# A macaron layer with two FFNs: more joint FFN blocks, token products last, theta per head, inverse roots without reciprocals

## The chip, the cores and the metric

The kernel runs on one NeuronCore of a Trainium2 chip. The metric is the device time of one execution in microseconds; smaller is better. Three runs of the kernel before gave 2110.48, 2112.5 and 2111.97 us (median 2111.97). All data is float32; large products are done in TensorE's `fp32r` format.

## The reference

One decoder layer on 1024 tokens of 1024 features. It adds half a SwiGLU FFN to `x`, then a mixer, then half a second FFN, and ends with an RMSNorm.

```python
x = x + 0.5 * swiglu(rms_norm(x, ffn1_norm), ffn1_w_gate, ffn1_w_up, ffn1_w_down)   # D_FF = 2816 = 22 x 128
x = x + hybrid_mixer(rms_norm(x, mix_norm), w_in, ...)
x = x + 0.5 * swiglu(rms_norm(x, ffn2_norm), ffn2_w_gate, ffn2_w_up, ffn2_w_down)
return rms_norm(x, final_norm)

def swiglu(h, w_gate, w_up, w_down):
    return (silu(h @ w_gate) * (h @ w_up)) @ w_down
```

The mixer projects `h @ w_in` to 3808 columns. Four HGRN2 heads of 128 (columns q, f, i, g) do gated linear recurrence in chunks of 64 tokens, each output normed over its head: `o * rsqrt(mean(o*o) + 1e-6)`. Eight RWKV-7 heads of 64 (columns r, k, v and low-rank columns for decay, `a` and gate) run a delta-rule recurrence; their key is divided by its length, `kk / max(sqrt(sum(kk*kk)), 1e-12)`, and their output is group-normed, `(y - mean) * rsqrt(var + 64e-5)`. Both halves are joined and multiplied by `w_out`. All mixing is causal.

## The kernel before

Features lie on the 128 partitions and tokens along the free dimension. The 1024 tokens are two blocks of `TB` = 512. Each large product is done in three passes (`mm3`, lines 101 to 103): weights and operands are split into a rounded part `hi` and a rest `lo` (`split`, lines 69 and 70: ScalarE rounds, VectorE subtracts), and `w.hi*x.hi + w.hi*x.lo + w.lo*x.hi` is summed in PSUM. Weights come from DRAM in pieces of 128 x 512 (`w_raw`), are split, and are used once or twice.

The order in time is:

1. `ffn_both`, FFN1. The first 10 of 22 FFN column blocks (`ALONE`) are done for token block 0 alone, the other 12 (`BOTH`) for both token blocks jointly by `unit`. A unit treats [gate, up] x [two halves of the features] x [two token blocks] as a 2 x 2 matrix product and does it with 7 half products instead of 8. It needs sums and differences of the weight pieces, made by VectorE (lines 287 to 298), and of the operands, made once per FFN by `Versions.first` and `Versions.rest`; the latter are `jobs`, taken one at a time from block 3 on. The down products of a group go to both token blocks, and `down` adds them onto the residual (line 459).
2. `project_in` for token block 0: first the token-major products (`tokens`, lines 587 to 589), which give the i columns and the 160 low-rank columns as tokens x columns, the low-rank part then transposed back; then 24 column products r, k, v and f, q, g (evacuated in line 648). From the sixth on, the first RWKV pairs are prepared (`early`).
3. `mixer` for block 0, in between the large products of what follows: `rwkv_pair` (keys, decays, gram matrices), `rwkv_solve` (a triangular inverse, theta, by VectorE), `rwkv_chain` (8 chunks one after the other), `rwkv_post` (group norm), twice, and four `hgrn_head`. It stores its outputs to DRAM (`od`).
4. `ffn` for block 1, its 10 blocks of FFN1 that were left out, then `project_in` and `mixer` of block 1.
5. For each token block: `project_out` (loads `od` by `out_operands`, multiplies by `w_out`, adds the parked residual) and `ffn` with all 22 blocks of FFN2 in six `GROUPS`. The final norm of block 0 is done in the middle of block 1's output projection; block 1's last group is done token-major by `Finish`, which norms and stores.

No order is written out by hand for the engines. A list scheduler orders the instructions of each engine by priority: a place in the program, moved ahead by `AHEAD` = 6000 for loads, splits and evacuations, by `SOON` = 20000 for the RWKV work, by `AHEAD - LATER` for the operand versions. All DMAs but a few go through SP's queue. Buffers are rings (`hp` for normed operands, `ft`, `w_raw`, `v` for operand versions, `sh`, `sr`, `po` for the mixers, PSUM rings `psf` 3, `hq` 2, `rq` 2, `ry` 1); rings of a later `stage` lie over those of the earlier one, in the order of their declaration.

An inverse root is `rsqrt` (lines 122 and 123: ScalarE square root, VectorE reciprocal); `rwkv_pair` has its own in lines 792 and 793. In a step of `rwkv_chain`, `z` is copied into a block-diagonal tile `zbd` by ScalarE (907) and VectorE (908), two products with theta and all 128 rows give `u` (913), and ScalarE copies it (914).

Of the kernel before, what the change touches and what calls it, by code (L numbers as in the profile page):

```python
# [15 lines left out]
P = 128  # L16
D = 1024
# [19 lines left out]
NTOK = 256  # L37
TOK_AT = 0
# [139 lines left out]

def ffn(E, xs, g, wgu, wdn, r=None, finish=None, groups=GROUPS, onto=None):

    nc = E.nc
    end = sum(groups[-1])
# [14 lines left out]
    def gate(pg, pu, half):  # L197
        with E.tc.high_priority(AHEAD):
# [16 lines left out]
    for f0, nf in groups:  # L215
        a = []
        last = finish and f0 + nf == NF
        if last:
            w_last = finish.weights(E, wdn, f0, nf)
        for f in range(f0, f0 + nf):  # L220
# [8 lines left out]
            a.append(gate(*late[:2], last))  # L229
            if wait and f == 1:  # L230
                late.append(product(f, 1))
                a.append(gate(*late[2:], last))
            late = []
        if last:
            finish(E, xs, a, w_last)
            return
# [10 lines left out]
    return xs  # L247
# [105 lines left out]
class Gate(Parts):  # L353


    def silu(self, t):
        with self.E.tc.high_priority(AHEAD):
            self.E.nc.scalar.activation(out=t, in_=t, func=AF.Silu)
# [6 lines left out]
    def c21(self, x):  # L365
        E, V = self.E, self.E.nc.vector
        with E.tc.high_priority(AHEAD):
            V.tensor_tensor(out=self.t0, in0=x, in1=self.t0, op=ALU.mult)
# [4 lines left out]
class Versions:  # L373
# [41 lines left out]
def ffn_both(E, x0, x1, g, wgu, wdn):  # L415


    nc = E.nc
# [31 lines left out]
    def gated(f):  # L450
        use = Gate(E)
# [12 lines left out]
    jobs = [lambda: r.append(rstd_of(E, x1))] + [lambda k=k: v.rest(x1, r[1], k) for k in range(HK)]  # L464
    ahead = None
    for f0, nf in ALONE:
        a = []
        for f in range(f0, f0 + nf):
# [6 lines left out]
            if f == 1:  # L475
                v.first(x0, r[0])
# [8 lines left out]
    for f0, nf in BOTH:  # L485
        a += [gated(f) for f in range(f0 + len(a), f0 + nf)]
        if f0 + nf < NF:
# [6 lines left out]
            continue  # L494
        for hb, xs in enumerate((x0, x1)):
            for d in range(KD):
                down(xs, d, wd(d, f0, nf), [h[hb] for h in a], "psf")


class Finish:  # L500
# [5 lines left out]
    def weights(self, E, wdn, f0, nf):  # L506
        nc = E.nc
        self.gain = []
        for h in range(2):
            t = E.ev.tile([P, TB + 1], F32, name="ev")[:, 0:TB]  # L510
            nc.sync.dma_start(out=t, in_=self.nf_row[:, h * TB:(h + 1) * TB].broadcast_to([P, TB]))
            self.gain.append(t)
        w = []
        with E.tc.high_priority(AHEAD):
            for h in range(2):
                for f in range(f0, f0 + nf):
                    raw = E.wraw.tile([P, 512], F32, name="w_raw")
                    nc.sync.dma_start(out=raw.rearrange("p (d c) -> p d c", c=P), in_=wdn[4 * h:4 * h + 4, :, f * P:(f + 1) * P].rearrange("d p c -> p d c"))
                    w.append(split(E, raw, E.sh.tile([P, TB], F32R, name="sh"), E.sr.tile([P, TB + 1], F32R, name="sr")[:, 0:TB]))
        return [w[:nf], w[nf:]]  # L520

    def __call__(self, E, xs, a, w):
        nc = E.nc
        E.idle = ["hq", "hq", "rq", "rq", "ry"]
        for t in range(TB // P):
# [3 lines left out]
            for h in range(2):  # L529
# [7 lines left out]
                sq = E.rs.tile([P, TB], F32, name="rs")  # L537
# [26 lines left out]
def project_in(E, b, xs, g, win, wtok, midway, early):  # L564
# [10 lines left out]
    def tokens(w_cols, n, banks, hooks={}):  # L575

        each = TB // P // len(banks)
        ps = [getattr(E, name).tile([P, TB], F32, name=name) for name in banks]
        ps = [p[:, i * n:(i + 1) * n] for p in ps for i in range(each)]
        for k in range(KD):  # L580
            if k in hooks:
                hooks[k]()
            w = load_piece(E, w_cols[:, k * n:(k + 1) * n])
            for t, p in enumerate(ps):
                x = h[k][:, t * P:(t + 1) * P]
                opens, closes = k == 0 and t % each == 0, k == KD - 1 and t % each == each - 1
                nc.tensor.matmul(p, x.hi, w.hi, start=opens, stop=False)
                nc.tensor.matmul(p, x.lo, w.hi, start=False, stop=False)
                nc.tensor.matmul(p, x.hi, w.lo, start=False, stop=closes)
        return ps  # L590

    def evacuate(p, t, c, dst):
        n = p.shape[1]
        e = E.ft.tile([P, TB], F32, name="ft")[:, 0:n]
        nc.scalar.activation(out=e, in_=p, func=AF.Copy, scale=rt[:, t:t + 1])
        nc.sync.dma_start(out=pd["i"][t * P:(t + 1) * P, dst:dst + n - c], in_=e[:, c:n])
        return e

# [4 lines left out]
    def rms_of_tokens():  # L603
        p = E.psf.tile([P, TB], F32, name="psf")[:, 0:4]
        for t in range(4):
            nc.tensor.matmul(p[:, t:t + 1], r[:, t * P:(t + 1) * P], E.ident[:, 0:1], start=True, stop=True)
        with tc.high_priority(AHEAD):
            nc.vector.tensor_copy(out=rt, in_=p)

    r = None  # L610
    rt = E.rw.tile([P, 4], F32, name="rt")
    first = tokens(wtok[:, 0:KD * NTOK], NTOK, ("hq", "hq"))
    second = tokens(wtok[:, KD * NTOK:], 512 + NLOW + NG - NTOK, ("rq", "rq", "ry", "psf"), {TOK_AT: rms, TOK_AT + 3: rms_of_tokens})
    lows = [E.psf.tile([P, TB], F32, name="psf") for _ in range(2)]
# [26 lines left out]
    for ci, name in enumerate(order):  # L641
# [13 lines left out]
        if ci == 5:  # L655
            early(pd, low)
# [634 lines left out]
```

## Time and profile before

| what | before |
|---|---|
| median of three runs | 2111.97 us |
| the profiled execution, its time and its span | 2111.52 us, 2108.6 us |
| TensorE busy | 2061.7 us, 11144 matmuls |
| VectorE busy | 1395.8 us, 2369 instructions |
| ScalarE busy | 954.3 us, 1562 instructions |
| mean granted TensorE clock | 0.995 |
| read from HBM | 197.77 MB |

The span goes from the first to the last instruction; the time adds what lies around it. A matmul's busy time is its latency, and matmuls overlap, so counts and starts of matmuls say more than busy times. Lines are those of the kernel before.

### The profile page before, as it was taken

How to read it: one execution, taken by the hardware profiler on the slowest of the kernel's cores; microseconds unless marked ns; L12 is line 12 of the kernel's file. 1: busy time of each engine (PE TensorE's matmuls, PEld its weight loads, DVE VectorE, ACT ScalarE, POOL GpSimd, SP SyncE). 2: the span in 40 equal slices, each digit the busy share in tenths (PEclk: the TensorE clock that was granted, in tenths of full speed). 3: DMA queues.
4: the chain of work that ended last, by engine and by line, in shares of the span. 5: the costliest groups of instructions: out<-in, count | busy, mean ns of one | idle time of the engine just before them, and what ended most of it. 6: DMA issues, size and time to landing. Idle time of an engine off the chain costs nothing.

```text
span 2108.6 us, 29995 instructions
## 1 busy us (share of the span) xinstructions
PE 2061.7 (98%) x11144; PEld 1674.6 (79%) x11144; DVE 1395.8 (66%) x2369; ACT 954.3 (45%) x1562; POOL 37.8 (2%) x68
## 2 busy tenths in 40 slices
PE   8999999999999999999999998999999999999998
PEld 6788888888877778776877776877888888888887
DVE  7876645455677978886677789966444675444553
ACT  6443423233556756544556556544332453322333
POOL 0000000001010000000000000000000000000000
PEclk9999999999999999999999999999999999999999
DMA  6332211213544543343645532433332453333331
GB/s 195 89 96 61 60 51 52 64 46 120 163 151 150 168 123 111 109 110 106 195 133 157 165 97 91 118 98 91 95 97 90 139 180 96 100 95 98 98 114 66
DMA packets 156962, 233.81 MB, mean 111 GB/s; under 512 B 36976, under 2 KB 54384, under 8 KB 156816
## 3 DMA queue, kind: packets, MB, share of 16 engines
q1 hardware_dynamic: 155952, 230.55, 36.5%
q8 instruction: 87, 1.43, 0.3%
q10 hardware_dynamic: 864, 1.36, 0.2%
q14 instruction: 59, 0.48, 0.1%
HBM read 197.77 MB, written 34.08 MB: 110 GB/s over the span
## 4 chain that ended last, share of the span: by engine, by line
PE 89%; DVE 5%; ACT 2%; issue 2%; DMA 1%; SPq 0%; ACTq 0%; DVEq 0%
PE psf L103 23%; PE psf L102 23%; PE psf L101 23%; PE hq L103 2%; PE hq L101 2%; PE hq L102 2%; PE rq L824 1%; DVE w_lo L70 1%; PE rq L102 1%; PE rq L103 1%; PE rq L101 1%; PE rq L913 1%; PE rq L917 1%; PE rq L906 1%; ACT w_hi L69 1%
## 5 line engine op out<-in xcount | busy, mean ns | idle before, releaser
L69 ACT CAST w_hi<-w_raw 128x512 fp32r<-128x512 f32 (+3 forms) x668 | 404.0, 606 | 875.4 <-PE psf L102 666.7
L70 DVE TENSOR_TENSOR w_lo<-w_raw,w_hi 128x512 fp32r<-128x512 f32 (+3 forms) x668 | 442.0, 666 | 190.7 <-ACT w_hi L69 187.9
L103 PE MATMUL psf<-h_hi,w_lo 128*128 128x512 f32 x1312 | 517.3, 395 | 7.9 <-DVE w_lo L70 7.9
L101 PE MATMUL psf<-h_hi,w_hi 128*128 128x512 f32 x1312 | 518.6, 395 | 3.5 <-ACT rs L122 2.2
L102 PE MATMUL psf<-h_lo,w_hi 128*128 128x512 f32 x1312 | 518.9, 396 | 0.0
L103 PEld LDWEIGHTS psf<-h_hi,w_lo 128*128 128x128 f32 x1312 | 247.0, 188 | 63.9 <-DVE w_lo L70 11.8
L101 PEld LDWEIGHTS psf<-h_hi,w_hi 128*128 128x128 f32 x1312 | 247.0, 188 | 57.7 <-ACT rs L122 2.7
L102 PEld LDWEIGHTS psf<-h_lo,w_hi 128*128 128x128 f32 x1312 | 247.1, 188 | 52.8 <-issue 1.9
L101 PE MATMUL psf<-v,w_hi 128*128 128x512 f32 x488 | 190.1, 389 | 1.6 <-ACT v L69 1.1
L103 PE MATMUL psf<-v,w_lo 128*128 128x512 f32 x488 | 189.9, 389 | 0.0
L102 PE MATMUL psf<-v,w_hi 128*128 128x512 f32 x488 | 189.9, 389 | 0.0
L101 PE MATMUL psf<-a_hi,w_hi 128*128 128x512 f32 x408 | 159.7, 392 | 0.5 <-ACT a_hi L69 0.5
L102 PE MATMUL psf<-a_lo,w_hi 128*128 128x512 f32 x408 | 159.4, 391 | 0.0
L103 PE MATMUL psf<-a_hi,w_lo 128*128 128x512 f32 x408 | 158.8, 390 | 0.0
L246 DVE SCALAR_TENSOR_TENSOR xp<-psf,xp 128x512 f32<-128x512 f32 x112 | 77.0, 689 | 79.5 <-PE psf L103 78.8
L101 PEld LDWEIGHTS psf<-v,w_hi 128*128 128x128 f32 x488 | 91.6, 188 | 21.5 <-ACT v L69 1.5
L102 PEld LDWEIGHTS psf<-v,w_hi 128*128 128x128 f32 x488 | 91.6, 188 | 19.1
L103 PEld LDWEIGHTS psf<-v,w_lo 128*128 128x128 f32 x488 | 91.6, 188 | 18.9
L101 PEld LDWEIGHTS psf<-a_hi,w_hi 128*128 128x128 f32 x408 | 76.4, 188 | 17.4 <-ACT a_hi L69 0.9
L102 PEld LDWEIGHTS psf<-a_lo,w_hi 128*128 128x128 f32 x408 | 76.6, 188 | 16.0 <-DVE a_lo L70 0.2
L103 PEld LDWEIGHTS psf<-a_hi,w_lo 128*128 128x128 f32 x408 | 76.5, 188 | 15.8
L209 DVE TENSOR_TENSOR ft<-psf,ft 128x512 f32<-128x512 f32 x50 | 34.4, 689 | 56.5 <-PE psf L103 56.4
(400 smaller groups left out, 2875.5 us busy)
## 6 DMA issues: line engine op xcount, KB each, us to landing
w_raw<-in_wgu_dram SPq DMA_DIRECT2D x304, 256.0 KB, 3.1
w_raw<-in_wd_dram SPq DMA_DIRECT2D x134, 256.0 KB, 2.7
w_raw<-in_win_dram SPq DMA_DIRECT2D x96, 256.0 KB, 3.0
w_raw<-in_wout_dram SPq DMA_DIRECT2D x32, 256.0 KB, 2.8
w_raw<-in_wd_dram SPq DMA_DIRECT2D x24, 192.0 KB, 2.3
park<-xp SPq DMA_DIRECT2D x16, 256.0 KB, 2.0
xp<-park SPq DMA_DIRECT2D x16, 256.0 KB, 3.5
ft<-od SPq DMA_DIRECT2D x16, 256.0 KB, 3.6
```

The costliest lines, as they stand in the source:

```text
L69: nc.scalar.copy(out=hi, in_=raw)
L70: nc.vector.tensor_tensor(out=lo, in0=raw, in1=f32(hi), op=ALU.subtract)
L101: E.nc.tensor.matmul(ps, w.hi, x.hi, start=start and i == 0, stop=False, **on)
L102: E.nc.tensor.matmul(ps, w.hi, x.lo, start=False, stop=False, **on)
L103: E.nc.tensor.matmul(ps, w.lo, x.hi, start=False, stop=(i == n - 1), **on)
L209: nc.vector.tensor_tensor(out=s, in0=pu, in1=s, op=ALU.mult)
L246: nc.vector.scalar_tensor_tensor(out=xs[d], in0=p, scalar=0.5, in1=xs[d], op0=ALU.mult, op1=ALU.add)
L824: PE.matmul(gps[hh][:, c, :], bk[r, c0 + c, :, :], g.ra[r, jj, c0 + c, :, :], start=True, stop=True)
L906: PE.matmul(z[r, jj, :], ra[r, jj, cc, 1, :], M[r, jj, :], start=False, stop=jj == 1, tile_position=(hh * C, hh * C))
L913: PE.matmul(u[C:P, jj, :], E.theta[:, jj, cc, :], E.zbd[:, jj, :, :], start=True, stop=True, tile_position=(0, C))
L917: PE.matmul(m[r, jj, :], bkt[:, cc, jj, r], uv[:, cc, jj, r], start=True, stop=True, tile_position=(0, hh * C))
```

## The change

- `ALONE` has 8 blocks instead of 10 and `BOTH` 14 instead of 12. FFN2 now uses the same scheme: token block 0 does its 8 blocks by `ffn` right after its output projection; then, in a stage of its own, the output projection of block 1 and `ffn_both` with block 1 as the first and block 0 as the second token block. Block 0's residual before FFN2 is stored to DRAM (`mid`) and loaded again for its operand versions; its inverse root `r` is kept. Block 0's final norm now comes between the last down products and `Finish`, whose group has 4 blocks instead of 3.
- The first stage declares its rings as `v, a, xb, wraw, ft` instead of `xb, ft, wraw, a, v`.
- In `project_in` the low-rank columns are done first and feature-major (two products with 64 and 96 output rows), and the token-major i products last, in two passes of two token tiles that load the weights each.
- In `rwkv_chain` theta is applied per head: four products of 64 x 64 instead of two with the block-diagonal tile; their result is copied half by ScalarE and half by VectorE.
- In the mixers' three norms `rsqrt_step` takes the place of root and reciprocal: logarithm, exponential, square, and one Newton step on VectorE. Its factor -0.5 is folded into constants (`onorm2`, `k_k2`) or the next operation.

```diff
-GROUPS = ((0, 4), (4, 4), (8, 4), (12, 4), (16, 3), (19, 3))
-ALONE = ((0, 4), (4, 4), (8, 2))
-BOTH = ((10, 4), (14, 4), (18, 4))
+ALONE = ((0, 4), (4, 4))
+BOTH = ((8, 4), (12, 4), (16, 2), (18, 4))
...
+def rsqrt_step(E, y, z, scratch):
+    A, V = E.nc.scalar, E.nc.vector
+    A.activation(out=y, in_=z, func=AF.Ln)
+    A.activation(out=y, in_=y, func=AF.Exp, scale=-0.5)
+    A.activation(out=scratch, in_=y, func=AF.Square)
+    V.tensor_tensor(out=z, in0=scratch, in1=z, op=ALU.mult)
+    V.scalar_tensor_tensor(out=y, in0=z, scalar=-3.0, in1=y, op0=ALU.add, op1=ALU.mult)
...
-    first = tokens(wtok[:, 0:KD * NTOK], NTOK, ("hq", "hq"))
-    second = tokens(wtok[:, KD * NTOK:], 512 + NLOW + NG - NTOK, ("rq", "rq", "ry", "psf"), {TOK_AT: rms, TOK_AT + 3: rms_of_tokens})
+    for i, (at, m, dst) in enumerate(((NG, NLOW, lraw), (0, NG, sgl))):
+        p = E.psf.tile([P, TB], F32, name="psf")[0:m]
+        for k in range(KD):
+            if k % 3 == 0:
+                w = load_piece(E, wtok[:, k * NL:min(k + 3, KD) * NL])
+            c = k % 3 * NL + at
+            if i == 0 and k == 1:
+                rms()
+            for n, (u, x) in enumerate(((w.hi, h[k].hi), (w.hi, h[k].lo), (w.lo, h[k].hi))):
+                nc.tensor.matmul(p, u[:, c:c + m], x, start=k + n == 0, stop=k == KD - 1 and n == 2)
... (after the 24 column products)
+    for two in ((0, 1), (2, 3)):
+        ps = [E.psf.tile([P, TB], F32, name="psf") for _ in two]
+        for k in range(KD):
+            w = load_piece(E, wtok[:, KD * NL + k * TB:KD * NL + (k + 1) * TB])
+            for t, p in zip(two, ps):
+                ... (three passes of 128 x 512)
...
-    rsqrt(E, sq, ss, P, E.eps)
+    z, sq, tmp = s2(), s2(), s2()
+    V.tensor_scalar(out=z, in0=ss, scalar1=1.0 / P, scalar2=EPS, op0=ALU.mult, op1=ALU.add)
+    rsqrt_step(E, sq, z, tmp)
...
-    A.activation(out=sq, in_=sq, func=AF.Sqrt)
-    V.reciprocal(out=sq, in_=sq)
+    z, sq, tmp = sq, tk(s2()), tk(s2())
+    rsqrt_step(E, sq, z, tmp)
...
-            A.copy(out=E.zbd[0:C, :, 0, :], in_=z[0:C])
-            V.tensor_copy(out=E.zbd[C:P, :, 1, :], in_=z[C:P])
+            A.copy(out=E.zs[0:C], in_=z[0:C])
+            V.tensor_copy(out=E.zs[C:P], in_=z[C:P])
...
-            for jj in range(2):
-                PE.matmul(u[C:P, jj, :], E.theta[:, jj, cc, :], E.zbd[:, jj, :, :], start=True, stop=True, tile_position=(0, C))
-            A.copy(out=uv[C:P, cc, :, :], in_=u[C:P])
+            for jj, hh, r in heads:
+                PE.matmul(u[r, jj, :], E.theta[r, jj, cc, :], E.zs[r, jj, :], start=True, stop=True, tile_position=(hh * C, hh * C))
+            A.copy(out=uv[C:P, cc, :, 0:C], in_=u[0:C])
+            V.tensor_copy(out=uv[C:P, cc, :, C:P], in_=u[C:P])
...
-    with stage(xb=8, ft=6, wraw=7, a=8, v=28):
+    with stage(v=28, a=8, xb=8, wraw=7, ft=6):
...
-        for b in range(NB):
-            o = out_operands(E, ods[b])
-            xs = project_out(E, o, parks[b], wout, lambda: b and final(b - 1, xs))
-            ffn(E, xs, E.n2, wgu2, wd2, finish=Finish(nf_row, out_last) if b + 1 == NB else None)
+        o = out_operands(E, ods[0], "hp")
+        xs = project_out(E, o, parks[0], wout, "xp")
+            mid = to_dram(xs, "mid")
+        xs, r = ffn(E, xs, E.n2, wgu2, wd2)
+    with stage(v=28, a=8, xb=8, wraw=7, ft=6, rw=1):
+        o = out_operands(E, ods[1], "v")
+        xb = project_out(E, o, parks[1], wout, "xb")
+        ffn_both(E, xb, xs, E.n2, wgu2, wd2, of_first, r, Finish(nf_row, out_last), lambda: final(0, xs))
```

More of the change, by code (lines that the diff above doesn't have):

```diff
@@ L195, in product, with gate @@
         return p
-    def gate(pg, pu, half):
+    def gate(pg, pu):
         with E.tc.high_priority(AHEAD):
@@ L214, in ffn @@
     late = []
-    for f0, nf in groups:
+    for f0, nf in ALONE:
         a = []
-        last = finish and f0 + nf == NF
-        if last:
-            w_last = finish.weights(E, wdn, f0, nf)
         for f in range(f0, f0 + nf):
@@ L450, in gated @@
     def gated(f):
-        use = Gate(E)
+        use = Gate(E, 0.5 if finish and f >= BOTH[-1][0] else None)
         unit(E, [wgu[f, :, j, i * TB:(i + 1) * TB] for j in range(2) for i in range(2)], v, use)
@@ L494, in ffn_both @@
             continue
+        if finish:
+            w_last = finish.weights(E, wdn, f0, nf)
         for hb, xs in enumerate((x0, x1)):
+            if finish and hb == 0:
+                continue
             for d in range(KD):
                 down(xs, d, wd(d, f0, nf), [h[hb] for h in a], "psf")
+        if finish:
+            then()
+            finish(E, x0, [h[0] for h in a], w_last)
 class Finish:
@@ L507, in weights @@
         nc = E.nc
[L508 to L512, printed above, removed]
+        t = E.v.tile([P, 2, TB], F32, name="v")
+        nc.sync.dma_start(out=t.rearrange("p h c -> p (h c)"), in_=self.nf_row.broadcast_to([P, D]))
+        self.gain = [t[:, h, :] for h in range(2)]
         w = []
@@ L573, in project_in @@
     pd = {"i": E.dram.tile([TB, 512], F32, name="pd_i")}
[L575 to L597, printed above, removed]
     def rms():
@@ L656, in project_in @@
             early(pd, low)
+    rt = E.rw.tile([P, 4], F32, name="rt")
+    p = E.psf.tile([P, TB], F32, name="psf")[:, 0:4]
+    for t in range(4):
+        nc.tensor.matmul(p[:, t:t + 1], r[:, t * P:(t + 1) * P], E.ident[:, 0:1], start=True, stop=True)
+    with tc.high_priority(AHEAD):
+        nc.vector.tensor_copy(out=rt, in_=p)
+    for two in ((0, 1), (2, 3)):
[3 more added lines that the diff above has]
+            for t, p in zip(two, ps):
+                x = h[k][:, t * P:(t + 1) * P]
+                nc.tensor.matmul(p, x.hi, w.hi, start=k == 0, stop=False)
+                nc.tensor.matmul(p, x.lo, w.hi, start=False, stop=False)
+                nc.tensor.matmul(p, x.hi, w.lo, start=False, stop=k == KD - 1)
+        with tc.high_priority(AHEAD):
+            for t, p in zip(two, ps):
+                e = E.ft.tile([P, TB], F32, name="ft")
+                nc.scalar.activation(out=e, in_=p, func=AF.Copy, scale=rt[:, t:t + 1])
+                nc.sync.dma_start(out=pd["i"][t * P:(t + 1) * P], in_=e)
     return low, sg, pd, ahead
@@ L993, in out_operands, with project_out @@
             nc.sync.dma_start(out=t, in_=od[k])
-            hi = E.hp.tile([P, TB], F32R, name="h_hi")
-            lo = E.hp.tile([P, TB], F32R, name="h_lo")
-            o.append(split(E, t, hi, lo))
+            if ring == "v":
+                o.append(part(E, t, ring))
+            else:
+                o.append(split(E, t, E.hp.tile([P, TB], F32R, name="h_hi"), E.hp.tile([P, TB], F32R, name="h_lo")))
     return o
-def project_out(E, o, xpark, wout, midway):
+def project_out(E, o, xpark, wout, ring):
     nc = E.nc
@@ L1066, in mixer_constants @@
     G.memset(E.theta, 0.0)
[L1067 to L1068 removed]
+    E.zs = k.tile([P, 2, C], F32, name="zs")
     wraw = E.sh.tile([P, TB], F32, name="sh")[0:64]
```

100 lines of the change are left out of this document (43 added, 57 removed).

## The prediction

> **What bounds the kernel now.** I read the page's parts 1, 2 and 4 first, then the timeline of the tensor engine where nothing disturbs it.
>
> ```profile
> span 2108.6 us, 29995 instructions
> PE 2061.7 (98%) x11144; PEld 1674.6 (79%) x11144; DVE 1395.8 (66%) x2369; ACT 954.3 (45%) x1562; POOL 37.8 (2%) x68
> PE   8999999999999999999999998999999999999998
> PE 89%; DVE 5%; ACT 2%; issue 2%; DMA 1%; SPq 0%; ACTq 0%; DVEq 0%
> 1849.65 0.39 PE L102 MATMUL psf<-h_lo,w_hi 128*128 128x512 f32 x1
> 1864.83 0.39 PE L103 MATMUL psf<-a_hi,w_lo 128*128 128x512 f32 x1
> 219.49 0.69 DVE L368 TENSOR_TENSOR ft<-psf,ft 128x512 f32<-128x512 f32 x1
> 238.53 0.69 DVE L368 TENSOR_TENSOR ft<-psf,ft 128x512 f32<-128x512 f32 x1
> ```
>
> TensorE is busy in every slice and holds 89% of the chain that ended last, so the question is how many matmuls go and which idle stretches come or go. The reader must not use the 0.39 us: that is one matmul's latency, and its neighbours overlap it. From 1849.65 to 1864.83 stand 68 matmuls in a row: 15.18 / 67 = 0.2266 us each. The two L368 rows are the ends of two joint units of FFN1, 19.04 us apart = 84 x 0.2267: a joint block runs at the pure matmul pitch.
>
> **1. Sixteen more joint blocks: -43.4 us.** A block of 128 FFN columns done for each token block alone takes 2 x 2 x 8 x 3 = 96 gate and up matmuls, 21.75 us; the joint unit takes 7 x 4 x 3 = 84, 19.04 us by the row above. The change makes 2 more in FFN1 (12 to 14) and 14 in FFN2 (none so far): 16 x 2.71 = 43.4. The down matmuls stay the same in number. Weight pieces and their splits become fewer (7 splits and 4 additions instead of 8 splits for a unit, one load of down weights for two products), and the evacuation grows a little.
>
> ```profile
> 40.00:60.00 20.00, 17.47 (x75) 13.56 (x74) 19.97 (x33) 13.79 (x24) 0.00 (x0) 1.00 0.33 93
> 60.00:80.00 20.00, 18.75 (x82) 14.88 (x81) 17.03 (x23) 9.15 (x13) 0.00 (x0) 1.00 0.27 79
> 120.00:140.00 20.00, 20.00 (x90) 16.57 (x89) 18.30 (x30) 9.82 (x17) 0.00 (x0) 1.00 0.31 92
> 340.00:360.00 20.00, 20.00 (x90) 16.57 (x89) 12.78 (x20) 9.20 (x16) 0.00 (x0) 1.00 0.21 54
> 2080.00:2108.00 28.00, 22.07 (x112) 17.72 (x110) 9.79 (x22) 11.17 (x26) 0.00 (x0) 0.98 0.20 75
> ```
>
> Columns: window, length, busy time of PE, PEld, DVE, ACT, POOL, granted clock, DMA share. In the joint stretch (340 to 360) VectorE has 7 of 20 us to spare, so the new units in FFN2 are hidden under TensorE. Where a joint FFN begins they are not: at 40 to 80 VectorE prepares the 16 operand versions and TensorE loses 2.53 + 1.25 = 3.8 us. FFN2 now gets such a beginning: **+3.8**. The first joint unit now follows block 7 rather than block 9, while at 120 to 140 VectorE was still 18.3 of 20 busy with the versions' last part: I take **+2** for each FFN, +4 (0, when the unit's first 5.4 us of products that need only the early versions cover it; 10, about one part's VectorE work, when not). In FFN2 that part also has to load the other block's `mid` tiles again and takes 5 of the 6 `ft` buffers; this lies within the same bound. The final norm of block 0 moves to the tail, beside the last token-major products, where DMA is 0.20 and VectorE a third busy: **+1**, 0 to 4.
>
> **2. Token products last, low-rank columns first: -4.6 and -2.**
>
> ```profile
> 544.42 0.80 PE L587 MATMUL hq<-w_hi,h_hi 128*128 128x256 f32 x2 [3.79 <-ACT h_hi L173]
> 579.36 0.40 PE L101 MATMUL hq<-h_hi,w_hi 128*128 128x512 f32 x1
> L829 PE MATMUL rq<-ident,t 128*128 128x128 f32 x64 | 9.7, 274 | 0.0
> 540.00:560.00 20.00, 15.89 (x105) 15.06 (x104) 15.69 (x28) 12.56 (x25) 0.18 (x1) 0.83 0.79 240
> ```
>
> Now: 34.94 us from the first token product to the first column product, in each of two blocks 69.9 (taken the same for the second). After: 48 narrow-output matmuls with 512 columns and 96 token matmuls with 512 columns, 144 x 0.2266 = 32.6, twice 65.3. The 16 transposes of the low-rank part go: at most 16 x 0.274 = 4.4, I take 2 because they overlap others. No new wait: the low products pass in 10.9 us, and their evacuation needs `r`, but the two borrowed banks carry two column products, 10.9 us, meanwhile.
>
> **3. The pools' order in the first stage: -3.8 us.** The 544.42 row shows TensorE idle for 3.79 us until ScalarE wrote `h_hi`. In the old order the new `hp` pool lies over `xb`, which the last down products still write and which then has to be stored. In the new order it lies over `v`, read last by the joint units; the split can run under the 96 last down products (21.8 us). If that cover fails the term is 0.
>
> **4. Theta per head: 0, -9 to +11.**
>
> ```profile
> 968.74 0.45 PE L906 MATMUL rq<-mst,ra 64*64 64x64 f32 x8
> 970.02 0.65 PE L913 MATMUL rq<-zbd,theta 128*64 128x128 f32 x4
> 969.29 0.26 ACT L907 COPY zbd<-rq 64x128 f32<-64x128 f32 x1 [0.52 <-PE rq L906]
> 969.58 0.29 DVE L908 COPY zbd<-rq 64x128 f32<-64x128 f32 x1 [1.01 <-ACT zbd L907]
> 970.70 0.37 ACT L914 COPY uv<-rq 64x256 f32<-64x256 f32 x1 [1.15 <-PE rq L913]
> ```
>
> Per step of the chain, 32 in all: the theta products take 0.65 us, and per head they have the shape of L906, 0.45: -0.20. Their copy, 0.37 on ScalarE alone, becomes one on ScalarE and one on VectorE. Side by side they take 0.29 (-0.28 a step, -9); one after the other, as L907 and L908 run on one PSUM tile, 0.58 (+0.01 a step). I take the latter, the nearest row; a VectorE that is busy when its copy comes adds up to half of a 0.69 us operation, 32 x 0.35 = +11.
>
> **5. No reciprocals: -4, 0 to -8.**
>
> ```profile
> L123 DVE RECIPROCAL po<-po 128x512 f32<-128x512 f32 x8 | 26.8, 3350 | 3.6 <-ACT po L122 3.6
> L123 DVE RECIPROCAL sh<-sh 128x512 f32<-128x512 f32 x8 | 26.7, 3343 | 1.7 <-ACT sh L122 1.7
> L793 DVE RECIPROCAL sr<-sr 128x512 f32<-128x512 f32 x8 | 26.7, 3338 | 1.0 <-ACT sr L792 1.0
> L941 DVE TENSOR_TENSOR po<-po 128x512 f32<-128x512 f32 x8 | 5.5, 689 | 0.0
> L797 DVE SCALAR_TENSOR_TENSOR sr<-sr,vec 128x512 f32<-128x512 f32 x8 | 6.0, 748 | 0.0
> L139 ACT ACTIVATE ft<-xp 128x512 f32<-128x512 f32 x56 | 33.8, 626 | 14.0 <-DVE ft L141 8.1 <-DVE xp L1012 3.8 <-DVE xp L246 1.6
> L686 ACT ACT_TABLE_LOAD x8 | 10.3, 1283 | 0.1
> L718 ACT ACT_TABLE_LOAD x6 | 7.7, 1283 | 0.1
> PE psf L103 <- DVE w_lo L70: 7.9, 8, 1.7
> ```
>
> VectorE loses 24 reciprocals of 3.34 and gains 24 x (0.69 + 0.75) + 16 x 0.69: 80.2 - 45.6 = 34.6 us less. What TensorE gets of that is bounded by its waits for a split weight piece, 7.9 us in all; I take half. ScalarE gains a second and a third pass (2 x 0.63) and, since L718's exponential reloads its table after L686's logarithm, one more load of 1.28: 24 x 2.54 = 61 us, on an engine that is 45% busy. The step is not shorter for the one who waits: 1.28 + 0.63 + 3.34 = 5.3 before, about 2 x 1.28 + 3 x 0.63 + 0.69 + 0.75 = 5.9 after (root, logarithm and square taken as long as L139's pass).
>
> The Trainium skill says in "ScalarE: Activation LUTs", section "Table sets: the hidden batching unit", that logarithm and exponential share a set, so the pair costs one load. By that rule ScalarE would do 24 x 1.28 = 31 us less and the sum would stay; the second block's mixers would end some 8 x 1.28 = 10 us earlier, and I would give the first rival 12 instead of 18 in 100. The L718 row speaks against it: the kernel pays a load there now.
>
> **6. The cover of the second block's mixers: +4, 0 to +25.** This is the term I know least.
>
> ```profile
> L758 SPq DMA_DIRECT2D od<-sh x8: 326/327/327, 776.9 to 1405.3; - x8
> L945 SPq DMA_DIRECT2D od<-po x8: 319/326/327, 809.5 to 1468.3; - x8
> 1181.93 0.69 DVE L648 TENSOR_TENSOR ev<-psf,rs 128x512 f32<-128x512 f32 x1
> L102 PE MATMUL psf<-h_lo,w_hi 128*128 128x512 f32 x209 | 86.2, 413 | 0.0
> L102 PE MATMUL psf<-a_lo,w_hi 128*128 128x512 f32 x62 | 24.1, 389 | 0.0
> 1181.00:1468.00 287.00, 281.17 (x2172) 217.50 (x2172) 229.57 (x426) 151.98 (x250) 3.88 (x5) 0.99 0.36 105
> od<-po SPq DMA_DIRECT2D x8, 256.0 KB, 2.1
> ft<-od SPq DMA_DIRECT2D x16, 256.0 KB, 3.6
> ```
>
> From the last column products (1181.9) to the mixers' last store (1468.3) TensorE issues 3 x (209 + 62) = 813 large matmuls, 184 us, between the mixers' small ones; they come from the first output projection and the first block's FFN2, which has plenty left at 1468. After the change the first block's FFN2 alone has only 8 blocks: 8 x 72 = 576 matmuls, with 192 of the output projection and the 96 token products moved there 864, 196 us. Nothing else can run until the second output projection gets its operands: store and load (2.1 + 3.6 us) and eight splits (8 x 0.69 on VectorE), 11 us, some 10 since the first heads are loaded before. So 196 against 184 + 10: the cover just holds, and with the mixers' jitter I take +4. SP's queue carries those loads ahead of the output weights, and both stand behind the last store.
>
> **Sum.** -43.4 + 3.8 + 4 + 1 - 4.6 - 2 - 3.8 + 0 - 4 + 4 = -45.0. The profiled execution took 2111.5 (span 2108.6 and 2.9 around it), 0.5 under the median shown: 2111.5 - 45.0 = 2066.5, so **2066 us**.
>
> **The rivals.** (a) The cover falls short. For it: the balance in 6 and VectorE busy 229.6 of 287 us there. Against it: of the 34.6 us that VectorE saves, those after 1181 (four heads, four norms and two pairs, 8 x 1.2 + 2 x 1.9 = 13.4, less 16 x 0.29 for theta copies) shorten the queue that the mixers wait in. A shortfall of 25 us in place of the 4 gives 2066 - 4 + 25, and a slow clock comes on top: in the 540 row, after 3.79 us idle, the clock is 0.83 over 20 us, 3.4 us lost. That is 2090, chance 18. The Trainium skill ("TensorE: Matmul & The Clock Gate", "Part 1: The HAM clock gate") has half clock after one idle window of about 3.4 us until about 3.4 us of work have passed, which would make that loss 1.7 and this rival 2089.
>
> (b) Slower than before, by the HGRN heads: they need the token products, which now come last. Those are 22 us of large products in a stretch where such products get 184 of 287 us, so the heads end 34 us later, at 1405 + 34 = 1439, still ahead of the 1468 of the RWKV norms. Should they be pushed behind all RWKV work instead, each us past the cover is a us of idle TensorE; from 45 + 4 - 3.4 = 46 us on, past 1468 + 46 = 1514, the kernel is slower than before: 2112 to 2130. Chance 5.
>
> (c) VectorE's relief counts for more: in the stretch from 1181 to 1468 the mixers' small matmuls and waits take 287 - 184 = 103 us; an eighth of it less in both blocks is 25 us, 2041. For it speaks VectorE's 80% there, against it that the waits for a split piece sum to only 7.9. Chance 17.
>
> (d) The change doesn't do in FFN2 what it does in FFN1, for lack of `ft` buffers or VectorE, and its joint blocks run at the alone pace: 14 x 2.71 = 38 back, 2104. The 340 row speaks against it; chance 3. The forecast has the other 57.
>
> **How the numbers follow.** 2066 is the likeliest case. Its own range, the ends of terms 1 to 6 that are not rivals and never all at one side: chain -9 to +11, reciprocals -4 to +4, beginnings -9 to +9, cover -4 to +10: 2050 to 2082. With (c) and the shortfalls up to 25 us the range is 2041 to 2091, leaving out (b), (d) and the rims of the others. 0.2% is 4.2 us, about what a measurement of this kernel can tell: (b) is slower, almost nothing falls within 4.2 us of 2112, everything else is faster: 0.93, 0.02, 0.05.
>
> **What would show it.** FFN2's units end 19.04 us apart with TensorE full (1); TensorE not idle for over 1 us ahead of block 0's first low-rank product (3); the theta copies staggered or side by side (4); no reciprocal in the mixers and about 24 more table loads (5); between the last `od` store of block 1 and the first product on it, TensorE busy (6). A clock under 1.00 and idle TensorE just ahead of the second output projection would make the prediction wrong upward; TensorE fuller than now through both mixers, downward.

## The result, and the profile after

The changed kernel takes 2131.1 us (median of four runs, 2130.0 to 2140.3) against 2111.2: ratio 1.0105, 95% interval 1.009 to 1.012. It is 20 us slower where 45 us less were forecast. Its profiled run is the longest of the four (2140.3), so the trace read here shows some 9 us more than the median.

The page's summary misleads: TensorE is 97% busy, against 98% before. What helps is to cut the span at two events, the first product on the low-rank operand (the mixers' recurrence begins; L779 before, L777 after) and the last `od` store (L756 the HGRN heads, L946 the RWKV norms). Rows of the lines' own lists (min/median/max ns, first and last start):

```profile
L779 PE MATMUL rq<-low,w x8: 477/483/501, 588.1 to 1274.7; 96*128 96x512 f32 x8
```
```profile
L777 PE MATMUL rq<-low,w x8: 472/480/502, 588.5 to 1317.7; 96*128 96x512 f32 x8
L756 SPq DMA_DIRECT2D od<-sh x8: 319/326/327, 877.3 to 1492.2; - x8
L946 SPq DMA_DIRECT2D od<-po x8: 319/326/327, 816.7 to 1518.0; - x8
```

The windows between these events (length, then busy time and number of instructions of PE, PEld, DVE, ACT and POOL, then the granted clock, the DMA share and GB/s), before and then after:

```profile
0.00:588.00 588.00, 570.66 (x2552) 473.36 (x2552) 364.72 (x571) 243.60 (x415) 14.17 (x29) 0.99 0.31 92
588.00:1468.00 880.00, 857.93 (x5790) 678.62 (x5791) 691.73 (x1278) 487.69 (x779) 23.60 (x40) 0.99 0.42 126
1468.00:2108.00 640.00, 633.14 (x2804) 522.60 (x2802) 339.38 (x522) 222.96 (x369) 0.00 (x0) 1.00 0.35 107
```
```profile
0.00:588.00 588.00, 573.91 (x2504) 468.84 (x2504) 383.32 (x598) 247.01 (x413) 12.88 (x26) 1.00 0.30 88
588.00:1518.00 930.00, 886.36 (x5810) 685.13 (x5811) 669.43 (x1342) 550.96 (x852) 27.85 (x41) 0.97 0.42 127
1518.00:2138.00 620.00, 606.98 (x2656) 497.71 (x2654) 381.61 (x590) 235.24 (x405) 0.00 (x0) 0.99 0.26 81
1760.00:2000.00 240.00, 240.00 (x1061) 198.72 (x1060) 125.70 (x191) 76.22 (x129) 0.00 (x0) 1.00 0.17 51
```

The part behind the mixers is 20 us shorter, and FFN2's joint blocks keep TensorE full there (last row). The part ahead is as long as it was. The mixers' span grew by 50 us, with VectorE's work down by 22 us and ScalarE's up by 63. No engine is full in that span: TensorE idles 44 of 930 us and runs at clock 0.97, VectorE is 72% busy. I take it for a chain of latencies with large products laid between; e4, e5 and e16 below test that. What part of the 50 us the lower clock has was not separated.

Each run below, cut in the same way (us; the median and ratio are of all its runs, the other columns of its profiled one; "ahead" to the first low-rank product, "span" to the later of the two last stores):

| run | median | ratio (95%) | ahead | last RWKV / HGRN store | span | behind |
|---|---|---|---|---|---|---|
| before | 2111.2 | | 588 | 1468 / 1405 | 880 | 640 |
| after | 2131.1 | 1.0105 (1.009-1.012) | 588 | 1518 / 1492 | 930 | 621 |
| e1 | 2122.6 | 1.0055 (1.004-1.007) | 589 | 1481 / 1502 | 914 | 621 |
| e2 | 2136.7 | 1.0128 (1.0113-1.0143) | 583 | 1490 / 1517 | 934 | 623 |
| e3 | 2129.4 | 1.0089 (1.0074-1.0104) | 584 | 1475 / 1512 | 928 | 618 |
| e4 | 2109.8 | 0.9996 (0.9987-1.0006) | 611 | 1492 / 1430 | 881 | 616 |
| e5 | 2076.4 | 0.9836 (0.9821-0.985) | 581 | 1459 / 1398 | 878 | 615 |
| e6 | 2165.0 | 1.0249 (1.0232-1.0266) | 610 | 1552 / 1485 | 942 | 615 |
| e7 | 2125.3 | 1.0065 (1.005-1.008) | 589 | 1470 / 1505 | 916 | 618 |
| e8 | 2156.0 | 1.02 (1.0174-1.0225) | 589 | 1520 / 1447 | 931 | 637 |
| e9 | 2133.3 | 1.0109 (1.0094-1.0124) | 588 | 1488 / 1426 | 899 | 644 |
| e10 | 2144.0 | 1.0158 (1.0141-1.0175) | 578 | 1468 / 1499 | 920 | 647 |
| e11 | 2140.0 | 1.0145 (1.013-1.0161) | 589 | 1498 / 1434 | 909 | 640 |
| e12 | 2070.2 | 0.9808 (0.9793-0.9823) | 582 | 1462 / 1401 | 880 | 606 |
| e13 | 2150.6 | 1.0195 (1.0178-1.0212) | 573 | 1469 / 1490 | 917 | 658 |
| e14 | 2130.2 | 1.0098 (1.0083-1.0113) | 588 | 1481 / 1454 | 893 | 649 |
| e15 | 2102.5 | 0.9966 (0.9953-0.9979) | 561 | 1458 / 1486 | 926 | 614 |
| e16 | 2067.0 | 0.9796 (0.9781-0.981) | 554 | 1459 / 1397 | 905 | 607 |

### The profile page after: what moved, and what is told of

It is laid out like the page before. It is cut to its first block, busy times and chain, and to the rows that moved or that the text cites. A ratio compares the mean times of both kernels' runs of the same rounds, so it can differ in the third digit from the quotient of the medians.

```text
span 2138.6 us, 29619 instructions
## 1 busy us (share of the span) xinstructions
PE 2067.2 (97%) x10968; PEld 1651.7 (77%) x10968; DVE 1434.4 (67%) x2529; ACT 1033.2 (48%) x1669; POOL 40.7 (2%) x67
## 3 DMA queue, kind: packets, MB, share of 16 engines
q10 hardware_dynamic: 864, 1.36, 0.2%
## 4 chain that ended last, share of the span: by engine, by line
PE 44%; DVE 4%; ACT 3%; issue 2%; DMA 1%; SPq 0%; DVEq 0%; ACTq 0%
PE psf L99 9%; PE psf L100 9%; PE psf L101 9%; PE hq L100 2%; PE hq L101 2%; PE hq L99 2%; PE rq L101 1%; PE rq L100 1%; PE rq L99 1%; DVE w_lo L68 1%; PE rq L822 1%; PE rq L911 1%; PE rq L916 1%; ACT L128 1%; PE rq L902 0%
## 5 line engine op out<-in xcount | busy, mean ns | idle before, releaser
L67 ACT CAST w_hi<-w_raw 128x512 fp32r<-128x512 f32 (+2 forms) x632 | 386.2, 613 | 791.5 <-PE psf L100 434.0
L68 DVE TENSOR_TENSOR w_lo<-w_raw,w_hi 128x512 fp32r<-128x512 f32 (+2 forms) x632 | 425.8, 675 | 176.4 <-ACT w_hi L67 167.2
L99 PE MATMUL psf<-v,w_hi 128*128 128x512 f32 x1072 | 419.4, 391 | 7.4 <-ACT v L67 5.0
L100 PE MATMUL psf<-v,w_hi 128*128 128x512 f32 x1072 | 419.0, 391 | 0.2 <-DVE v L68 0.2
L101 PE MATMUL psf<-v,w_lo 128*128 128x512 f32 x1072 | 418.4, 390 | 0.0
L101 PE MATMUL psf<-h_hi,w_lo 128*128 128x512 f32 x704 | 281.5, 402 | 6.8 <-DVE w_lo L68 6.6
L99 PE MATMUL psf<-h_hi,w_hi 128*128 128x512 f32 x704 | 282.7, 402 | 3.5 <-DVE ev L624 1.5
L100 PE MATMUL psf<-h_lo,w_hi 128*128 128x512 f32 x704 | 282.0, 401 | 2.1 <-DVE h_lo L68 2.1
L99 PEld LDWEIGHTS psf<-v,w_hi 128*128 128x128 f32 x1072 | 202.0, 188 | 53.5 <-ACT v L67 7.2
L100 PEld LDWEIGHTS psf<-v,w_hi 128*128 128x128 f32 x1072 | 202.1, 189 | 42.9 <-DVE v L68 1.3
L99 PEld LDWEIGHTS psf<-h_hi,w_hi 128*128 128x128 f32 x704 | 134.2, 191 | 33.6 <-issue 3.1
L99 PE MATMUL hq<-a,w_hi 128*128 128x512 f32 x288 | 112.3, 390 | 1.0 <-ACT w_hi L67 1.0
L100 PE MATMUL hq<-a,w_hi 128*128 128x512 f32 x288 | 112.1, 389 | 0.0
```

The lines of the kernel that those rows point to most:

```text
L67: nc.scalar.copy(out=hi, in_=raw)
L68: nc.vector.tensor_tensor(out=lo, in0=raw, in1=f32(hi), op=ALU.subtract)
L99: E.nc.tensor.matmul(ps, w.hi, x.hi, start=start and i == 0, stop=False, **on)
L100: E.nc.tensor.matmul(ps, w.hi, x.lo, start=False, stop=False, **on)
L101: E.nc.tensor.matmul(ps, w.lo, x.hi, start=False, stop=(i == n - 1), **on)
```

## The experiments

### A wait found first: lraw in the ring of the heads (e1, e2, e3)

In the trace of after, the second block's low rank is evacuated at 1021, but its shift (`sh<-ev`, the tile `lraw`) runs at 1059.57: `lraw` takes one of the six tiles of ring `sh`, and the first block's last HGRN heads, late, hold them. I took that wait and the longer chain steps for the whole loss.

```
e2:  -    lraw = E.sh.tile([P, TB], F32, name="sh")[0:NLOW]
     +    lraw = E.rw.tile([NLOW, TB], F32, name="lraw")
e1:  theta, zs and the copies of u as in the kernel before;   e3: both
```


> After's kernel with before's theta: one block-diagonal product per pair and one ScalarE copy. Theory S (steps): theta per head costs about 1 us in each of the 32 chain steps (a clean step 4.03 us before, 5.3 to 5.8 after, because the eight products are cut in two groups with large products between them), and the recurrent path sets the end of both mixers; the four chains then last 42, 32, 42, 31 us as before and not 48, 48, 51, 46. Only the second block's two chains lie on the path if the block starts late for another reason: 2131 - 24 = 2107, 2095 to 2118. Theory R (ring): the second block's recurrence starts late by a tile it waits for; the start stays near 1060: 2131 - 5, 2118 to 2133. Theory C (plain shortage of large products): the idle time only moves, 2125 to 2135.

> After's kernel with the raw low-rank rows (lraw) in a tile of their own in place of one of the six of the ring sh, which the late HGRN heads of the first block hold until 1059. Theory R: the second block's low rank is ready at about 1030, 35 us earlier, and the whole recurrence of that block with it: 2131 - 35 = 2096, 2088 to 2112. Theory S: the start is earlier but the chains stay long and the first block's HGRN heads, pushed on, collide with them: 2120, 2110 to 2131. Theory C: 2125 to 2135, since what is idle is idle for lack of large products.

> Both edits of the two kernels before. Theories S and R together: the second block's recurrence starts 35 us earlier and lasts 24 us less, then TensorE has no more waits to lose than before's kernel had: 2131 - 55 = 2076, 2066 to 2092. Theory C: over 2110.

The wait, in after's timeline, and the same shift and the last stores in e2:

```profile
1059.57 0.71 ACT L659 ACTIVATE sh<-ev,mu 64x512 f32<-64x512 f32 x1
1065.16 0.47 PE L777 MATMUL rq<-low,w 96*128 96x512 f32 x1 [1.51 <-DVE low L568]
```
```profile
1021.09 0.72 ACT L659 ACTIVATE lraw<-ev,mu 64x512 f32<-64x512 f32 x1
L756 SPq DMA_DIRECT2D od<-sh x8: 319/326/1047, 875.9 to 1517.3; - x8
L946 SPq DMA_DIRECT2D od<-po x8: 320/326/327, 815.3 to 1490.0; - x8
```

The shift came 38 us earlier and RWKV's last store 28 us earlier. The last head came 25 us later (1492 to 1517) and took its place as the end: theory R falls as the cause of the loss, though the wait was real. e1's time lies in the range of theory R, but for another reason: RWKV ends 37 us earlier (1481), and the heads, now at 1502, are the end. So it gained 8.5 us and no more. e3, both edits together, gained 1.7 us where 55 were hoped for.

### What the joint blocks bring (e4, e5, e12, e16)

e4 has theta, roots and token products as before, so only the joint blocks and the pools' order are left of the change. The others build on it:

```
e5:   FFN1: ALONE ((0,4),(4,4),(8,2)), BOTH ((10,4),(14,4),(18,4)); FFN2 as in after
e12:  e5, and in ffn_both the row factor handed over is no job of its own:
      -    jobs = [lambda: r.append(r1 or rstd_of(E, x1))] + [...rest...]
      +    jobs = [...rest...]; insert the rstd job only if r1 is None
e16:  e12 with FFN1: ALONE ((0,4),(4,4),(8,4)), BOTH ((12,4),(16,2),(18,4))
```


> Only the joint blocks and the new order of the pools are left of the change: theta, the inverse roots and the token products stand as before. Theory C (the first block's FFN2 with 8 blocks instead of 22 is too little to lay beside the mixers): 2105 or more, the stretch of the mixers with 40 us more of idle TensorE. Theories S and R (the slow parts are theta and the late heads): the sixteen joint blocks bring their 43 us less some 15 for the start of the joint FFN2: 2111 - 43 + 15 = 2083, 2070 to 2095.

> The kernel with the joint blocks alone (old theta, old roots, token products first), with FFN1 back at 12 joint blocks and FFN2 at 14. Theory M (the mixers' span is a serial length): time is what lies ahead of the first low-rank operand (584 us before, 607 in the kernel with the joint blocks alone), the mixers' span from there to the last store (884 and 885) and what lies behind (640 and 616). FFN1's two extra joint blocks put 22 us ahead of the mixers and take 33 us of products out of a span that does not get shorter. So with 12: 585 + 885 + 616 + 3 = 2089, 2080 to 2097. Theory C2 (what is short is the cover of the second block's mixers, FFN2's 8 alone blocks): no gain, 2105 to 2115, and idle TensorE ahead of the second output projection.

> The kernel with joint blocks in FFN2 alone (2076), and the first of the jobs ahead of FFN2's joint blocks no longer the empty one (the row factor handed over): each of the four that build the versions comes one block earlier, at the third, fourth, fifth and sixth block in place of the fourth to seventh. Theory J (the 8.3 us of idle TensorE at 1640 to 1660, at FFN2's first joint unit, is that order): 2076 - 7 = 2069, 2066 to 2072. Rival (the versions are late for VectorE or for the buffers of the ring v, not for their order): 2074 to 2079.

> The same 2070 kernel with ten joint blocks in FFN1 in place of twelve (fourteen: 610 us ahead of the mixers, twelve: 581). Two blocks of the second half move into the mixers' span, 33 us of large products. Theory M (the first block's mixers last 446 us from their first low-rank product to the second block's, whether 8 or 10 alone blocks lie beside them): if there is room for 12, the start falls to 555 and the time to 2045; if TensorE is already full beside them with 10, the stretch grows to 475 or more and the time is 2070 - 27 + 33 = 2076, 2070 to 2085. In the kernel with 8, the idle TensorE of 960 to 1080 was 33 us above before's, just the two blocks that were gone, so I expect 2076.

Windows of e4, with the stretch 960 to 1080 last; the same stretch of before; windows of e5; the mixers' span of e16; and the stretch of FFN2's first joint unit, 1620 to 1640, in e5 and in e12:

```profile
0.00:610.00 610.00, 595.59 (x2672) 493.98 (x2672) 384.87 (x605) 253.68 (x431) 13.34 (x29) 1.00 0.30 89
610.00:1492.00 882.00, 833.36 (x5629) 660.03 (x5629) 676.28 (x1250) 475.05 (x757) 24.33 (x40) 0.97 0.41 125
960.00:1080.00 120.00, 101.14 (x857) 83.96 (x857) 55.26 (x96) 46.36 (x86) 2.69 (x4) 0.82 0.31 92
```
```profile
960.00:1080.00 120.00, 113.77 (x738) 93.35 (x736) 81.81 (x133) 63.60 (x116) 3.52 (x6) 0.97 0.50 156
```
```profile
0.00:581.00 581.00, 568.75 (x2552) 472.15 (x2552) 364.54 (x573) 244.48 (x415) 13.46 (x29) 1.00 0.32 93
581.00:1459.00 878.00, 853.97 (x5773) 674.61 (x5773) 691.34 (x1278) 486.24 (x779) 23.80 (x40) 0.99 0.43 129
1459.00:2074.00 615.00, 604.25 (x2651) 496.74 (x2651) 380.39 (x588) 232.35 (x400) 0.00 (x0) 0.99 0.26 82
```
```profile
554.00:1459.00 905.00, 884.87 (x5917) 699.61 (x5916) 701.30 (x1289) 497.36 (x792) 23.81 (x39) 1.00 0.43 129
```
```profile
1620.00:1640.00 20.00, 15.66 (x53) 10.73 (x52) 14.26 (x23) 8.62 (x16) 0.00 (x0) 0.83 0.29 79
```
```profile
1620.00:1640.00 20.00, 20.00 (x90) 16.58 (x89) 12.88 (x21) 8.72 (x15) 0.00 (x0) 1.00 0.35 104
```

The joint blocks alone bring nothing, and without FFN1's two they bring 34.6 us (2111.0 to 2076.4 in the same comparison). A block of FFN1 made joint runs for both token blocks ahead of the mixers: 2 x 72 x 0.2266 - 2.71 = 29.9 us instead of 72 x 0.2266 = 16.3. That is 13.6 us more each and 27 for two (measured 611 - 581 = 29). The second half's 2 x 72 products, 33 us, vanish from among the first block's mixers, and these do not end sooner: from first low-rank product to the second block's it is 446 us in e4 (to 1056.6) and 447 in before and e5. What was left there is an emptier TensorE (101 of 120 us, at clock 0.82), which cost the stretch nothing. e16 shows the other side: with two more blocks in that stretch it grows to 472 us, TensorE busy 118 of the 120 us from 960 to 1080, and 25 of the 28 us that the start gains go back. That is less than the 33 us expected, so its time lies below the range given for a full TensorE; still, e16 and e12 can't be told apart, their intervals overlap. So the mixers set this stretch with 8 and with 10 alone blocks (446 and 447 us), and with 12 it grows.

e4's time is the one of theory C, a lack of cover beside the second block's mixers, but that theory is wrong in its place: e5 has the same 8 alone blocks of FFN2 and its span is 878. e12 takes 6 us more off, behind the mixers (615 to 606): the empty first job had pushed the versions one block late, and TensorE waited at FFN2's first joint unit. In e5 it issues 53 matmuls from 1620 to 1640, where a full stretch has 90, as in e12. Of the versions that beat both kernels (e5, e12, e15, e16), e12 and e16 are the fastest.

### Theta per head (e8, e9)

```
e8:  before + theta, zs and the copies of u as in after
e9:  e8, and   -  A.copy(out=E.zs[0:C], in_=z[0:C]); V.tensor_copy(out=E.zs[C:P], in_=z[C:P])
               +  A.copy(out=E.zs, in_=z)
```


> The kernel before with theta per head as its only change. Theory S: steps of about 5 us instead of 4, on the path of both blocks' chains; 32 steps of 1 us, two thirds of them on the path: 2111 + 21 = 2132, 2120 to 2145. Theory C (steps are long in the kernel after because the large products beside them are short or badly placed, not because of theta): 2108 to 2115.

> The kernel before with theta per head, and z copied to zs by one ScalarE instruction of 128 rows in place of a ScalarE and a VectorE half. Theory S2 (the split copies are what theta per head costs: the first of the eight u products goes with ScalarE's half, then large products stand in TensorE's order until VectorE's half is there): the u products fall from 1.13 to 1.6 us to 0.45 and the copies from 0.58 to 0.4; a step loses 0.9 us, 32 steps 29 us, two to four quarters of it on the path: 2156 - 22 = 2134, 2122 to 2142. Theory N (eight small products cost the time by their number, however they are copied): 2148 to 2160.

Rows of one step in the timeline of after (where a product of two operands in f32 has two records), and of one in e9:

```profile
973.09 0.26 ACT L905 COPY zs<-rq 64x128 f32<-64x128 f32 x1 [0.17 <-PE rq L904]
973.38 0.29 DVE L906 COPY zs<-rq 64x128 f32<-64x128 f32 x1
973.41 0.32 PE L911 MATMUL rq<-zs,theta 64*64 64x64 f32 x2
973.67 0.44 PE L731 MATMUL hq<-ident,sh 128*128 128x128 f32 x2
973.86 0.48 PE L99 MATMUL psf<-a_hi,w_hi 128*128 128x512 f32 x1
974.17 0.40 PE L100 MATMUL psf<-a_lo,w_hi 128*128 128x512 f32 x1
974.50 0.44 PE L911 MATMUL rq<-zs,theta 64*64 64x64 f32 x6
```
```profile
965.84 0.45 PE L906 MATMUL rq<-mst,ra 64*64 64x64 f32 x8
966.39 0.27 ACT L907 COPY zs<-rq 128x128 f32<-128x128 f32 x1
966.88 0.45 PE L912 MATMUL rq<-zs,theta 64*64 64x64 f32 x8
967.92 0.33 PE L917 MATMUL rq<-uv,bkt 128*64 128x64 f32 x2
968.72 0.39 PE L917 MATMUL rq<-uv,bkt 128*64 128x64 f32 x5
970.23 0.45 PE L906 MATMUL rq<-mst,ra 64*64 64x64 f32 x8
```

In the kernel before, `z` was copied in two halves too, but each product read both, so the products stood together. Per head, the first head's product goes as soon as ScalarE's half is there; the next needs VectorE's half, and TensorE's order has other products in between. From the first u product to the last it is 1.5 us here (the median of the 32 steps is 1.36, and 0.65 before), although the products alone are 0.45.

Theta per head costs 45 us by itself, more than theory S allowed. From the first u product of a chain to that of its last step, the four chains take 144 us together in before, 172 in e8 and 152 in e9. With one copy the eight products stay together at 0.45, the step is 4.39 us (before's clean steps: 4.03), and some 22 of the 45 us come back, as theory S2 said. The m products are still cut (967.92, 968.72), since u goes in two copies. But by these sums, which leave out each chain's last step, the steps hold 28 of e8's 45 us and 8 of the 24 that e9 keeps; where the rest lies is not shown.

### The roots (e7, e11, e14)

```
e7:  after with rsqrt (Sqrt, reciprocal) in heads, pairs and norms
e11: before with rsqrt_step in all three;   e14: before with rsqrt_step in the heads alone
```


> After's kernel with the Sqrt and the reciprocals of before in the mixers. Theory A (the two table loads and three ScalarE passes of a root, 24 times, lengthen the mixers' path): 2131 - 10, 2115 to 2125. Theory V (the reciprocals' 35 us on VectorE come back, and VectorE is 74% busy in the mixers): 2131 + 8, 2133 to 2145. Neither: within 4 us of 2131.

> The kernel before with the inverse roots by logarithm, exponential and a Newton step as its only change. Theory V (VectorE's 35 us help): 2100 to 2107. Theory A (two table loads and three passes on ScalarE lengthen each root, 8 heads, 8 norms and 8 pairs): 2115 to 2125. In the kernel after, the old roots gave 6 us less, which speaks for A: 2117.

> The kernel before with the new inverse roots in the eight HGRN heads alone, the old ones in the pairs and the norms. Theory P (a root costs time where it lies on the recurrent path, in the pairs, 5.6 us before and 7.4 after, and the norms, 4.4 and 6.6; the heads have 60 us of slack at the end): 2110, 2106 to 2114. Rival Q (more passes on ScalarE slow everything, a third of the 24 roots costs a third of 30 us): 2118 to 2125.

The pair's root, before and after (first of eight each; the table load begins the step):

```profile
L792 ACT ACT_TABLE_LOAD  x7: 1283/1283/1283, 603.9 to 1134.3; - x7
L793 DVE RECIPROCAL sr<-sr x8: 3295/3346/3355, 606.8 to 1292.8; 128x512 f32<-128x512 f32 x8
```
```profile
L127 ACT ACT_TABLE_LOAD  x23: 1283/1283/1283, 606.8 to 1506.7; - x23
L128 ACT ACT_TABLE_LOAD  x24: 1283/1283/1283, 608.8 to 1509.2; - x24
L131 DVE SCALAR_TENSOR_TENSOR sr<-sr x8: 681/683/684, 613.0 to 1337.7; 128x512 f32<-128x512 f32 x8
```

From 603.9 to 610.1 it was 6.2 us; from 606.8 to 613.7 it is 6.9. Over the eight pairs, from the end of the clamp to the root, the median goes from 5.6 to 7.4 us in e11, and in the norms, table load included, from about 5.4 to 6.7. The span grows by 28 us and the time by 30, so VectorE's relief (31 us less work in e11) buys nothing: theory A in its direction, at more than twice its price.

That pairs and norms lie one behind the other would give 8 x 1.8 + 8 x 1.3 = 25 us, but no run has the new roots in them alone, and e14 speaks against that account and refutes theory P: roots in the heads alone, which end 27 us ahead of the last store, cost 21 us. 12 of them lie in the span, where the second block's first low-rank product comes 11 us later, and 9 behind it, where 2843 matmuls are left instead of 2804. The first block's last head is stored no later than in before (950 and 952), the second block's 48 us later. Whether that is ScalarE's queue or TensorE's fixed order, in which a waiting head product holds up what stands behind it, stays open. e7, the old roots put back into after, gains 6 us: RWKV ends 48 us earlier (1470), and the heads, at 1505, are the end.

### The token products (e6, e10, e13, e15)

```
e6:  after with before's project_in;   e10: before with after's project_in
e13: e10 with the token products behind column 12 of 24 (all r, k, v);   e15: e12 with e13's project_in
```


> After's kernel with before's order, token products first. Theory H (token products last make the HGRN heads late, and the heads end last in both blocks): the heads are stored about 90 us earlier and no longer set the end; the start of the mixers goes back from 588 to 607, the mixers' span from 930 to 905: 2131 + 19 - 25 = 2125, 2115 to 2131. Theory S (the chain's steps alone): the heads are not on the path, 2131 + 19 = 2150, 2138 to 2155.

> The kernel before with the low-rank columns first and the token products last as its only change. The mixers start some 18 us earlier (from 584 to 566) and, if heads end late as in the kernel after (90 us later than before), the second block's heads end at about 1495 in place of 1405 and the mixers' last store with them. Large products are plenty there (FFN2's 22 alone blocks), so theory K (with cover, time is TensorE's work, 4 us of transposes less): 2100 to 2110. Theory M (the mixers' span, however covered, sets the time): 2111 - 18 + 27 = 2120, 2112 to 2130.

> The kernel before with the low-rank columns first, and the token products behind the twelve r, k and v columns, ahead of the f, q and g columns, in place of last. Theory H (the 34 us of the token products last are the HGRN heads' lateness: last head stored at 1499 in place of 1405, behind the last RWKV store at 1468): the heads end ahead of 1468 again, the mixers' span falls from 920 back to about 885, and with the earlier start (578 in place of 588) the time is 2110 - 10 + 5 = 2105, 2098 to 2115. Rival L (the new low-rank products and what they displace on VectorE and in the buffers cost it, wherever the token products stand): 2130 to 2146.

> The kernel with joint blocks in FFN2 alone and the versions one block earlier (2070), with the low-rank columns first and the token products behind the r, k and v columns. Theory H: the mixers start some 10 us earlier and last as long: 2060, 2053 to 2068. Rival L: 2085 or more, as in the kernel before with the token products last.

The first products of the second block's first head, before and in e13, and the load of its token operand in e13:

```profile
L703 PE MATMUL hq<-sh x16: 222/223/243, 1189.1 to 1189.6; 128*64 128x32 f32 x16
```
```profile
L691 PE MATMUL hq<-sh x16: 222/223/243, 1248.8 to 1249.2; 128*64 128x32 f32 x16
1172.95 0.43 SPq L679 DMA_DIRECT2D sh<-pd_i  x1
```

By itself the new order costs 34 us: the start gains 10, the heads end 94 us later and set the end. That was more than either theory of e10 allowed.

Want of the token products is not the whole of it, as theory H had it: in e10 the second block's first operand lands only at 1251, but in e13 it is loaded from 1173 on and the head's first products still run at 1249. They stand behind the input projection in TensorE's order: they come at the evacuation of its last column or a few us ahead of it, in before (1189 and 1195.7) as in e13 (1249 and 1249.5). With the token products behind the low rank, that end lies 54 us later, though the recurrence does not: its third chain starts at 1196 in before and at 1201 in e13. So in before this head runs beside that chain, and in e13 it begins behind it. Moving the products to the middle changes nothing in that, so e13 and e15 both lose, by 41 us against before and 32 against e12.

In after the same move paid: e6, with the tokens first, is 34 us slower than after, slower than both its theories had it. There RWKV, with the new theta and roots, ends last (1552 against 1485), so the earlier start (588 in place of 610) counts and the heads' delay does not. In the profiled runs the start takes 22 us more, the span 12 more, and what lies behind 5 less.

So the parts do not add up: alone, theta, order and roots lengthen the span by 51, 40 and 28 us; together, in after, it is 50 longer (the joint blocks alone leave it as it was, 881 in e4). RWKV and the heads run side by side, and the span takes the longer. They also hold each other up: in e2 RWKV ends 28 us earlier than in after and the heads 25 later, in e1 it is 37 and 10.

## Why the prediction was wrong

The runs split the miss into three parts: FFN2's blocks and the pools brought -34.6 us (e5), FFN1's two blocks +33.4 (e5 to e4), and theta, roots and the token order together +21.3 (e4 to after). Their sum is the +20 measured.

- **Term 1** (-43.4 and +4): for the fourteen blocks of FFN2 the sum came right, in part by luck. From their terms, 14 x 2.71 = 38 less 3.8, 2 and 1, with 3.8 for the pools, 35 us were due and e5 gave 34.6. But behind the mixers it gained 25 us where 31 were reckoned, and the rest came ahead of them (7 instead of 3.8) and in the span (2). The beginning was under-priced: the first joint unit lost 37 of 90 matmuls in 20 us, 8 us by the pitch of 0.2266, not 2, and the order of the jobs made that (e12, 6 us in the time). FFN1's two blocks were the first failed step: -5.4 reckoned, +33.4 measured (e4 against e5). The sum took every product as TensorE time on the path, and the second half's products lay in a stretch that the mixers set.
- **Term 2** (-4.6 and -2, "No new wait"): +34 alone. It counted products and looked for waits at the low-rank columns; the HGRN heads, behind the projection in TensorE's order, were priced only in rival (b).
- **Term 3** (-3.8): right in its mechanism. The wait of 3.79 us ahead of block 0's projection is gone, and e5 reaches its first low-rank product 7 us earlier with as many matmuls (2552); TensorE is never idle for over 0.9 us in the 100 us ahead of it.
- **Term 4** (0, -9 to +11): +45 alone. The copies run staggered, as I took them, and the products are short, as I took them. What the sum lacked is that products which each need one of two copies, on two engines, fall into two groups with fillers between; e9, with one copy, gave some 22 us back.
- **Term 5** (-4): +30 alone. The work was counted well: in e11 25 more table loads (98 to 123; 24 forecast), 56 us more of ScalarE (61) and 31 less of VectorE (34.6). The step that failed is that this work was priced by TensorE's waits for a split weight. "The step is not shorter for the one who waits" was the right remark with 0.6 us to it, but the sum gave it nothing; measured, it is 1.3 to 1.8 us each for the norms and pairs, and the heads' roots, which no term saw on the path, cost 21 us alone (e14).
- **Term 6** (+4): right where it looked. With 8 alone blocks of FFN2 the second block's mixers are covered (e5). The shortage was beside the first block's, where FFN1's two blocks had been.
- **Rival (b)** named the heads pushed late, and the time lies just past the end of its 2112 to 2130. That it came so near is luck: its mechanism is half of what happened. In after the heads end at 1492, not 1439, and RWKV itself ends at 1518, not 1468.
- **What would show it**: FFN2's units came at full pitch, and the first low-rank product came earlier than with the old token order (588 against e6's 610); the sign that I named for a miss upward, idle TensorE at a lower clock just ahead of the second output projection, did not (19.8 of 22 us busy up to 1522, clock 1.00): the loss lies in the span ahead of it.

## What to carry to other kernels

Before pricing a change by the work it removes, cut the span at the events that start and end a latency-bound stretch, and ask of every removed product in which part it lay: work laid beside a serial chain is free as long as it fits there, and moving it ahead of the chain is paid in full. In such a chain price an edit by what the next instruction waits for, not by busy time: once each product needed only one of two copies on two engines, the group of products was cut in two, and the step lost far more than the 0.2 us that the products save. When two chains run side by side, the costs of single parts don't add; test each alone and together.

## What the runs showed of the hardware

A ScalarE copy of 128 x 128 from PSUM takes 0.27 us and one of 64 x 128 takes 0.26, so halving the rows saved nothing here. The exponential after the logarithm reloaded its table in 24 of 24 roots (the L128 row, 1283 ns each), 21 of them with nothing or a single cast or copy on ScalarE in between: the rule that the Trainium skill gives in "ScalarE: Activation LUTs", section "Table sets: the hidden batching unit", that the two share a set, does not hold in this trace. The granted clock was lower where TensorE was thinly covered: 0.82 in e4 with TensorE busy 101 of 120 us, against 0.97 in before at 114 of 120. The stretch of the mixers around it was as long in both (446 and 447 us).
